# Values of two attention groups made token by token in an fp32 encoder layer, and a weight stream in smaller pieces

## The chip, the core and the metric

The kernel runs on one core of a Trainium2 chip. The core has five engines that run side by side, each with its own fixed list of instructions: TensorE (PE, matrix products), VectorE (DVE), ScalarE (ACT), GpSimd (POOL) and SyncE (SP, which here issues transfers). They wait for each other by semaphores. The metric is the time of one execution on the device in microseconds (us); lower is better.

## What is computed

One layer of a bidirectional encoder over 512 tokens of width 1024, all in fp32. The reference, cut to what the change touches and what ends the kernel:

```python
h = layer_norm(x, ln0_g, ln0_b)
proj = h @ w_in[l] + b_in[l]              # gates B, C, conv input H, and q, k, v
q, k, v = (proj[...].reshape(bsz, seq, N_GROUPS, HEADS_PER_GROUP, HEAD_DIM) for ...)
for g, (window, dil) in enumerate(GROUPS):     # (128,1), (512,4), (2048,16); 8 heads of 64 each
    outs[g], lses[g] = dilated_window_attention(q[:, :, g], k[:, :, g], v[:, :, g], dil, window // (2 * dil), slopes[g])
wts = softmax(stack(lses))                      # the three groups' outputs are merged by their denominators
y_b = sum(wts * outs) @ w_b[l]
mix = (g_a * y_a + g_b * y_b) @ w_o[l] + b_o[l]
h = layer_norm(ALPHA * h + mix, ln1_g[l], ln1_b[l])
f = gelu(dwconv3(a, ffn_conv_w[l]) + ffn_conv_b[l]) * gte      # a, gte = h @ w_up + b_up
h = layer_norm(ALPHA * h + f @ w_down[l] + b_down[l], ln2_g[l], ln2_b[l])
```

## The kernel before

**Products.** An fp32 product is made of three matmuls (`mm3`, L313 to L315): both operands are split into a high and a low part, `hi` and `lo`, and hi·hi, hi·lo and lo·hi are added up in PSUM. `unit` makes 128 features of all 512 tokens: 8 steps of 128 input features, three matmuls each, 24 matmuls of 512 columns.

**Weights.** All weights are one stream of chunks of up to 2048 columns by 128 partitions. `load` (L241) issues a chunk's transfer on SP's queue into one of 2 `raw` buffers; `split` (L250) lets ACT copy it to `hi` (L261) and DVE subtract that copy to get `lo` (L263), 1024 columns at a time (the first two chunks' `lo` are made on POOL). `hi` and `lo` have 3 buffers each, of a chunk's full size. `chunk` splits the chunk that is wanted and the one after it, and loads one more.

**Order.** Each engine's list is arranged when the kernel is built, by a scheduler of the framework that follows the program's order where operands and buffers let it; a buffer that is still being read holds back the instruction that writes it, and what stands behind that one on its engine.

**Attention.** First the tokens are normalised, two tiles of 128 at a time, transposed to features (`hT`) and split. `in_units` then lists the projection in blocks of 128 features: for each of 4 pairs of heads and each of 3 groups a block of queries, keys and values. After each block, `slot` (L597) does a few steps of attention that are due: scores (`Job.a`), scaling by the merge's weights (`Job.b`), transposes of the scores (`Job.b2`), sums over keys (`Job.c`). The values of a block come out with features on partitions, but the sums want keys there: `evac_qkv` copies them to `vT` on ACT (L396 to L399), and `transpose_v` transposes them in four parts on PE (L406), copies the result to a high part (L409) and subtracts for the low part (L410).

**The end.** The gated MLP runs in two parts of the hidden features, with two halves of 512 output columns each. In the last (part 1, half 1), the three chunks of `w_down`, in the stream the numbers 79, 80 and 81, are all kept (`ws`), and the four rows (tiles of 128 tokens, `hb0` to `hb3`) are done one after the other: 11 steps `f11` to `f21` of products, an addition to the row (L809), statistics (L810 and `ln_finish`, L286 to L294), the norm in two steps (L815, L816) and the output's transfer (L817). The last row is done in two parts of 256 columns.

Of the kernel before, what the change touches and what calls it, by code (L numbers as in the profile page):

```python
# [5 lines left out]
F32 = mybir.dt.float32  # L6
# [5 lines left out]
P = 128  # L12
# [66 lines left out]
def lay_out_weights(w):  # L79
    """The weights as one stream of [128, columns] pieces; only moves elements."""  # L80
# [9 lines left out]
    for name, key, cols in chunk_plan():  # L90
        if name == "in":
            c = [block(w_in, units[key + i][3] * P, P) for i in range(2)]
        elif name == "wa":
# [41 lines left out]
def distance_tables():  # L135
    """-(distance) of query (partition) and key (column), MASKED where not attended to."""
# [10 lines left out]
def build(tc, x, wst, colt, dist, rows, out):  # L147
# [3 lines left out]
    with ExitStack() as ctx:  # L151
        pool = lambda name, bufs=1, **k: ctx.enter_context(tc.tile_pool(name=name, bufs=bufs, **k))
        const = pool("const")
        wraw = pool("wraw", 2)
        whl = pool("whl", 3)
        blkp = pool("blk", 25)
# [43 lines left out]
        def first_raw(i, c):  # L200
            if i not in raws:
                raws[i] = wraw.tile([P, 2048], F32, tag="raw", name=f"raw{i}")
            src = wst[i * P * 2048 : (i + 1) * P * 2048].rearrange("(p c) -> p c", p=P)
            first_load(raws[i][:, c : c + 1024], src[:, c : c + 1024])
# [18 lines left out]
        # keys of a pair of heads, block diagonal: rows of head h are zero outside of [:, h]  # L223
# [17 lines left out]
        def load(i):  # L241
# [3 lines left out]
            t = wraw.tile([P, 2048], F32, tag="raw", name=f"raw{i}")  # L245
            src = wst[int(offs[i]) : int(offs[i + 1])].rearrange("(p c) -> p c", p=P)
            nc.sync.dma_start(out=t[:, :n], in_=src)
            raws[i] = t

        def split(i):  # L250
# [5 lines left out]
            lo = whl.tile([P, 2048], F32R, tag="lo", name=f"lo{i}")  # L256
            step = 512 if i == 0 else 1024
            starts = (0, 1024, 512, 1536) if i == 0 else range(0, n, step)
            for c in starts:
                part = slice(c, min(c + step, n))  # L260
                nc.scalar.activation(hi[:, part], raws[i][:, part], AF.Copy)  # L261
                eng = nc.gpsimd if i < 2 else nc.vector
                eng.tensor_tensor(lo[:, part], raws[i][:, part], f(hi[:, part]), op=ALU.subtract)  # L263
            splits[i] = (hi, lo)
# [17 lines left out]
        def ln_finish(sts_, name):  # L282
# [4 lines left out]
            # 1/sqrt(v): the square root's table, then one Newton step  # L287
# [29 lines left out]
        def unit(o, w, c0, rhs, t0=0, t1=512):  # L317
            """o[128 features, tokens] = the block of weights at column c0, times rhs."""
# [43 lines left out]
        def nat(ap):  # L362
            """Token columns in the order (r, i) as seen in a tile whose columns are tokens 4i + r."""
# [48 lines left out]

        class Job:
            """Two heads times 512 columns of scores: a query tile and its window of 256 keys
            (group 0), or two residue classes of 128 queries and as many keys."""
# [69 lines left out]
            def c(self):  # L485
                """Adds to the sums over keys; rows of one head are of use in its own columns."""
                p, g, n = self.key
                v = vv[p, g]
# [351 lines left out]
```

## Time and profile before

| | |
|---|---|
| time, median of 3 runs | 1008.33 us (1007.52 to 1009.56) |
| span of the one profiled execution | 1004.4 us |
| PE busy | 974.7 us, 97% of the span, 4729 matmuls |
| DVE busy | 551.0 us, 55% |
| ACT busy | 398.2 us, 40% |
| POOL busy | 70.2 us, 7% |
| read from HBM, written | 93.84 MB, 2.15 MB |

The time of a run holds a few microseconds that the profiled span does not. Busy shares are means over stages that are limited by different engines. In the rows further down, "out<-in" names the tiles that an instruction writes and reads, L is the line of the kernel, and what stands after "idle before" or in brackets is the time the engine stood still and what ended it.

### The profile page before, as it was taken

The numbers are of one execution on the slowest core, as the hardware profiler recorded it, in microseconds if no ns is written. First come the engines' busy times: TensorE is split into PE (matmuls) and PEld (weight loads), VectorE is DVE, ScalarE is ACT, GpSimd is POOL, SyncE is SP. The second block draws the span as 40 slices with busy tenths as digits, with TensorE's granted clock in tenths as the row PEclk, the third lists the DMA queues.
The fourth block names the chain that finished last, engine by engine and source line by source line (L and its number), as shares of the span: only waits on it lengthen the run. The fifth ranks groups of instructions, "written<-read, shape, count | busy, mean of one in ns | idle before, by whom it ended". The sixth has DMA issues, their size and how long they took to land.

```text
span 1004.4 us, 11766 instructions
## 1 busy us (share of the span) xinstructions
PE 974.7 (97%) x4729; PEld 821.6 (82%) x4729; DVE 551.0 (55%) x863; ACT 398.2 (40%) x679; POOL 70.2 (7%) x161
## 2 busy tenths in 40 slices
PE   7999999999999999999999997799999999999996
PEld 7988888888888888888888886688888888888885
DVE  7856658657675445322355769664542345445256
ACT  4655564564543333233343223254442234444220
POOL 4000000000000000000000304400000000000000
PEclk9999999999999999999999997799999999999998
DMA  6322322122322212225243420232232322321402
GB/s 231 127 87 85 83 81 70 58 85 84 85 85 85 84 59 110 84 84 206 87 138 110 171 84 6 80 126 84 87 112 74 107 103 89 121 84 73 157 1 84
DMA packets 23462, 96.74 MB, mean 96 GB/s; under 512 B 9200, under 2 KB 9584, under 8 KB 13680
## 3 DMA queue, kind: packets, MB, share of 16 engines
q1 hardware_dynamic: 14256, 89.60, 25.6%
q0 software_dynamic: 1728, 6.29, 1.8%
q10 hardware_dynamic: 7424, 0.10, 0.4%
q8 instruction: 37, 0.61, 0.3%
q14 instruction: 17, 0.14, 0.0%
HBM read 93.84 MB, written 2.15 MB: 96 GB/s over the span
## 4 chain that ended last, share of the span: by engine, by line
PE 86%; DVE 8%; DMA 2%; ACT 2%; issue 1%; ACTq 0%; DVEq 0%
PE ps_acc L313 15%; PE ps_acc L314 15%; PE ps_acc L315 15%; PE ps_s L313 5%; PE ps_s L315 5%; PE ps_s L314 5%; PE ps_u L313 5%; PE ps_u L314 5%; PE ps_u L315 5%; PE ps_pt L313 4%; PE ps_pt L315 4%; PE ps_pt L314 4%; DMA s<-st 1%; DVE h1T L310 1%; PE ps_pt L479 1%; DVE h1T L309 1%
## 5 line engine op out<-in xcount | busy, mean ns | idle before, releaser
L263 DVE TENSOR_TENSOR lo<-raw,hi 128x1024 fp32r<-128x1024 f32 (+1 forms) x160 | 190.6, 1211 | 185.1 <-ACT hi L261 183.5
L261 ACT ACTIVATE hi<-raw 128x1024 fp32r<-128x1024 f32 (+1 forms) x166 | 166.6, 1033 | 231.0 <-PE ps_acc L314 67.5
L313 PE MATMUL ps_acc<-hT,hi 128*128 128x512 f32 (+1 forms) x512 | 198.6, 388 | 1.2 <-DVE kbd L392 0.9
L314 PE MATMUL ps_acc<-hT,hi 128*128 128x512 f32 (+1 forms) x512 | 196.7, 384 | 0.1
L315 PE MATMUL ps_acc<-hT,lo 128*128 128x512 f32 (+1 forms) x512 | 196.5, 384 | 0.0
L313 PEld LDWEIGHTS ps_acc<-hT,hi 128*128 128x128 f32 x512 | 96.5, 189 | 20.4 <-PE ps_pt L479 1.6
L315 PEld LDWEIGHTS ps_acc<-hT,lo 128*128 128x128 f32 x512 | 96.4, 188 | 19.2
L314 PEld LDWEIGHTS ps_acc<-hT,hi 128*128 128x128 f32 x512 | 96.5, 189 | 17.7 <-DVE hT L310 0.3
L460 ACT ACTIVATE S<-S,nm 128x128 f32<-128x128 f32 (+2 forms) x96 | 40.1, 419 | 54.3 <-DVE nm L458 47.5
L566 DVE SCALAR_TENSOR_TENSOR cv<-fp,cols,cv 128x512 f32<-128x512 f32 x22 | 16.5, 752 | 72.2 <-ACT cv L565 72.2
L314 PE MATMUL ps_acc<-h1T,hi 128*128 128x512 f32 (+1 forms) x96 | 38.3, 398 | 10.5 <-DVE h1T L310 5.9
L313 PE MATMUL ps_acc<-h1T,hi 128*128 128x512 f32 (+1 forms) x96 | 37.3, 389 | 3.2 <-DVE h1T L309 3.2
L315 PE MATMUL ps_acc<-h1T,lo 128*128 128x512 f32 (+1 forms) x96 | 37.1, 387 | 0.0
L314 PE MATMUL ps_s<-h1T,hi 128*128 128x512 f32 (+1 forms) x96 | 36.3, 378 | 0.0
L313 PE MATMUL ps_s<-h1T,hi 128*128 128x512 f32 (+1 forms) x96 | 36.3, 378 | 0.0
L315 PE MATMUL ps_s<-h1T,lo 128*128 128x512 f32 (+1 forms) x96 | 36.2, 377 | 0.0
L314 PE MATMUL ps_u<-h1T,hi 128*128 128x512 f32 (+1 forms) x96 | 35.7, 372 | 0.0
L315 PE MATMUL ps_pt<-h1T,lo 128*128 128x512 f32 (+1 forms) x96 | 35.7, 372 | 0.0
L314 PE MATMUL ps_pt<-h1T,hi 128*128 128x512 f32 (+1 forms) x96 | 35.7, 372 | 0.0
L313 PE MATMUL ps_u<-h1T,hi 128*128 128x512 f32 (+1 forms) x96 | 35.7, 372 | 0.0
L313 PE MATMUL ps_pt<-h1T,hi 128*128 128x512 f32 (+1 forms) x96 | 35.7, 372 | 0.0
L315 PE MATMUL ps_u<-h1T,lo 128*128 128x512 f32 (+1 forms) x96 | 35.7, 372 | 0.0
(371 smaller groups left out, 1945.7 us busy)
## 6 DMA issues: line engine op xcount, KB each, us to landing
raw<-wst SPq DMA_DIRECT2D x76, 1024.0 KB, 4.8
raw<-wst SPq DMA_DIRECT2D x4, 768.0 KB, 4.2
x<-x SPq DMA_DIRECT2D x4, 512.0 KB, 6.4
raw<-wst SPq DMA_DIRECT2D x4, 512.0 KB, 8.5
hb<-x POOLq DMA_DIRECT2D x4, 512.0 KB, 4.4
out<-hb SPq DMA_DIRECT2D x7, 256.0 KB, 2.1
ln_g<-rows POOLq DMA_DIRECT2D x3, 512.0 KB, 4.2
ln_b<-rows POOLq DMA_DIRECT2D x3, 512.0 KB, 5.4
```

Of the source, the lines that this page charges most:

```text
L261: nc.scalar.activation(hi[:, part], raws[i][:, part], AF.Copy)
L263: eng.tensor_tensor(lo[:, part], raws[i][:, part], f(hi[:, part]), op=ALU.subtract)
L309: nc.vector.tensor_copy(dst[:, 0, c0:c1], t)
L310: nc.vector.tensor_tensor(dst[:, 1, c0:c1], t, f(dst[:, 0, c0:c1]), op=ALU.subtract)
L313: nc.tensor.matmul(o, ah, bh, start=start, stop=False)
L314: nc.tensor.matmul(o, ah, bl, start=False, stop=False)
L315: nc.tensor.matmul(o, al, bh, start=False, stop=stop)
L460: nc.scalar.activation(v, v, AF.Exp, bias=nm[:, j : j + 1], scale=0.125, accum_out=dn[:, j : j + 1])
L479: nc.tensor.transpose(pt[:, j * P : (j + 1) * P], self.pe[:, j * P : (j + 1) * P], ident)
L566: nc.vector.scalar_tensor_tensor(a, u[:, 128:640], col(c + step), a, op0=ALU.mult, op1=ALU.add)
```

## The change

Four things. The values of groups 1 and 2 no longer come from blocks of features: `values` holds 128 tokens of `hT` still and moves 512 weight columns through, so that a group's values for all 8 heads come out with tokens on partitions, 4 tiles for each group. Their weights are two chunks `vt` for each group, behind the 4th and the 6th chunk pair of the projection (`V_AFTER`). `evac_values` adds a bias that is broadcast over partitions (`vbias`, loaded once on POOL's queue), copies and subtracts; nothing is transposed. Second, `raw` becomes 3 buffers of 1024 columns, `lo` becomes 5 buffers of 1024 (`Pieces` finds the piece for a column); `hi` keeps 3 buffers of 2048. A chunk of 2048 columns is loaded in two transfers. Third, `slot` counts in `ready` when a pair's sums are due, and takes newly made scores (`late`) at once rather than from the next slot on. Fourth, there are slots for the new tiles, and one more at the values of group 0 from the second pair on.

```diff
 def in_units():
...
             for kind, base in (("q", BLK_Q), ("k", BLK_K), ("v", BLK_V)):
-                units.append((kind, p, g, base + g * 4 + p))
+                if kind != "v" or g == 0:
+                    units.append((kind, p, g, base + g * 4 + p))
...
+V_AFTER = {4: 1, 6: 2}
...
-    out = [("in", i, 2048) for i in range(0, len(in_units()), 2)]
+    out = []
+    for i in range(0, len(in_units()), 2):
+        out.append(("in", i, 2048))
+        if i in V_AFTER:
+            out += [("vt", (V_AFTER[i], kh), 2048) for kh in range(2)]
...
+class Pieces:
+    def __init__(self, tiles):
+        self.tiles = tiles
+    def __getitem__(self, at):
+        rows, cols = at
+        t = self.tiles[cols.start // 1024]
+        c = cols.start % 1024
+        assert c + cols.stop - cols.start <= 1024
+        return t[rows, c : c + cols.stop - cols.start]
...
-        wraw = pool("wraw", 2)
+        wraw = pool("wraw", 3)
         whl = pool("whl", 3)
-        blkp = pool("blk", 25)
+        blkp = pool("blk", 28)
...
-            t = wraw.tile([P, 2048], F32, tag="raw", name=f"raw{i}")
             src = wst[int(offs[i]) : int(offs[i + 1])].rearrange("(p c) -> p c", p=P)
-            nc.sync.dma_start(out=t[:, :n], in_=src)
-            raws[i] = t
+            raws[i] = []
+            for c in range(0, n, 1024):
+                t = wraw.tile([P, 1024], F32, tag="raw", name=f"raw{i}")
+                nc.sync.dma_start(out=t[:, : min(1024, n - c)], in_=src[:, c : min(c + 1024, n)])
+                raws[i].append(t)
...
-            lo = whl.tile([P, 2048], F32R, tag="lo", name=f"lo{i}")
+            los = [whl.tile([P, 1024], F32R, tag="lo", name=f"lo{i}", bufs=5) for _ in range(0, n, 1024)]
...
+        vbias = blk(F32, (2, 512), "vbias")
+        nc.gpsimd.dma_start(out=vbias.rearrange("p a b -> p (a b)"), in_=vrow.partition_broadcast(P))
+        def values(g, j, ws):
+            o = ps("acc")
+            ts = slice(j * P, (j + 1) * P)
+            for k in range(KT):
+                w, b = ws[k // 4], slice(k % 4 * 512, k % 4 * 512 + 512)
+                mm3(o, hT[k][:, 0, ts], hT[k][:, 1, ts], w[0][:, b], w[1][:, b], k == 0, k == KT - 1)
+            return o
+        def evac_values(g, j, o):
+            a = f32t("vsum")
+            nc.vector.tensor_tensor(a, o, vbias[:, g - 1], op=ALU.add)
+            t = blk(F32R, (2, 4, P), f"vt{g}{j}")
+            nc.scalar.activation(t[:, 0], a.rearrange("p (a b) -> p a b", a=4), AF.Copy)
+            nc.vector.tensor_tensor(t[:, 1], a.rearrange("p (a b) -> p a b", a=4), f(t[:, 0]), op=ALU.subtract)
+            vtok[g, j] = t
...
-            if sums and sums[0].key[0] in cs and wait[0] == 0:
+            if sums and ready[sums[0].key[0]] <= wait[0]:
...
+            scores.extend(late)
+            late.clear()
             if scores:
...
-                    wait[0] = 3
+                    ready[p] = wait[0] + 3
...
-            wait[0] = max(0, wait[0] - 1)
-            scores.extend(late)
-            late.clear()
+            wait[0] += 1
...
             slot()
+            if kind == "v" and a0 > 0:
+                slot()
...
+            if n - 1 in V_AFTER:
+                g = V_AFTER[n - 1]
+                ws = [chunk("vt", (g, kh)) for kh in range(2)]
+                for j in range(4):
+                    o = values(g, j, ws)
+                    slot()
+                    evac_values(g, j, o)
```

Three places of the order are shown; the number behind a name tells tiles of one name apart, and the lines of the changed kernel are other ones (L342 to L344 for L313 to L315, L868 for L809, L874 for L815, L292 for L263).

PE at the end, before: the last products of row 0 (`ps_acc`) with the last chunk's `hi81` and `lo81`, and the first of row 1 (`ps_s`).

```order
L315 MATMUL ps_acc_7193<-hi81_7185,f20_6933 128x512
L313 MATMUL ps_acc_7193<-hi81_7185,f21_7006 128x512
L314 MATMUL ps_acc_7193<-lo81_7186,f21_7006 128x512
L315 MATMUL ps_acc_7193<-hi81_7185,f21_7006 128x512
L313 MATMUL ps_s_7246<-hi79_7125,f11_6276 128x512
L314 MATMUL ps_s_7246<-lo79_7126,f11_6276 128x512
L315 MATMUL ps_s_7246<-hi79_7125,f11_6276 128x512
```

PE at the end, after: the last part of row 3 (`ps_acc_7594`), and in it the last pairs of row 0 (`ps_acc_7399`), 1 (`ps_s`), 2 (`ps_pt`) and of the first part of row 3 (`ps_u`).

```order
L342 MATMUL ps_acc_7594<-hi79_7324,f14_6667 128x256
L343 MATMUL ps_acc_7594<-lo79_7326,f14_6667 128x256
L344 MATMUL ps_acc_7594<-hi79_7324,f14_6667 128x256
L343 MATMUL ps_acc_7399<-lo81_7392,f21_7199 128x512
L344 MATMUL ps_acc_7399<-hi81_7390,f21_7199 128x512
L343 MATMUL ps_s_7452<-lo81_7392,f21_7199 128x512
L344 MATMUL ps_s_7452<-hi81_7390,f21_7199 128x512
L343 MATMUL ps_pt_7505<-lo81_7392,f21_7199 128x512
L344 MATMUL ps_pt_7505<-hi81_7390,f21_7199 128x512
L343 MATMUL ps_u_7558<-lo81_7392,f21_7199 128x256
L344 MATMUL ps_u_7558<-hi81_7390,f21_7199 128x256
L342 MATMUL ps_acc_7594<-hi80_7379,f15_6743 128x256
```

Before, a row's three matmuls with `f21` stand together and the next row follows. After, a row's last two stand behind those that read `lo79` last.

DVE at the end, before: the split of the last chunk, and row 0 (`hb0`).

```order
L263 TENSOR_TENSOR lo81_7186<-raw81_7183,hi81_7185 128x1024
L263 TENSOR_TENSOR lo81_7186<-raw81_7183,hi81_7185 128x512
L809 TENSOR_TENSOR hb0_4330<-hb0_4330,ps_acc_7193 128x512
L810 BN_STATS l20st_7191<-hb0_4330 128x6
L286 BN_AGGR l20mv_7229<-l20st_7191 128x2
L289 TENSOR_SCALAR l20mv_7229<-l20mv_7229 128x1
L815 SCALAR_TENSOR_TENSOR hb0_4330<-hb0_4330,l20mv_7229,ln2_g_7173 128x512 x2
L804 BN_STATS l22st_7297<-hb2_4474 128x6
L290 RECIPROCAL l20mv_7229<-l20mv_7229 128x1
```

DVE at the same place after:

```order
L292 TENSOR_TENSOR lo80_7381<-raw80_7333,hi80_7379 128x1024
L774 TENSOR_TENSOR hb3_4643<-hb3_4643,ps_u_7205 128x512
L292 TENSOR_TENSOR lo81_7391<-raw81_7386,hi81_7390 128x1024
L292 TENSOR_TENSOR lo81_7392<-raw81_7388,hi81_7390 128x512
L868 TENSOR_TENSOR hb0_4418<-hb0_4418,ps_acc_7399 128x512
L868 TENSOR_TENSOR hb1_4493<-hb1_4493,ps_s_7452 128x512
L869 BN_STATS l20st_7397<-hb0_4418 128x6
L869 BN_STATS l21st_7450<-hb1_4493 128x6
L315 BN_AGGR l20mv_7435<-l20st_7397 128x2
L868 TENSOR_TENSOR hb2_4568<-hb2_4568,ps_pt_7505 128x512
L318 TENSOR_SCALAR l20mv_7435<-l20mv_7435 128x1
L874 SCALAR_TENSOR_TENSOR hb0_4418<-hb0_4418,l20mv_7435,ln2_g_7375 128x512 x2
```

The `lo81` piece that was made ahead of row 0 is now in two tiles, and rows 0 to 2 follow each other directly, where before row 0 was finished first.

DVE at the start, before: statistics of the second pair of token tiles (`l01mv`), their norm (`x2`, `x3`), the third chunk's `lo2`, and the first features' split (`hT0`).

```order
L289 TENSOR_SCALAR l01mv_357<-l01mv_357 128x2
L290 RECIPROCAL l01mv_357<-l01mv_357 128x2
L291 TENSOR_TENSOR l01mv_357<-l01mv_357 128x2
L292 TENSOR_TENSOR l01mv_357<-l01mv_357 128x2
L293 TENSOR_SCALAR l01mv_357<-l01mv_357 128x2
L294 TENSOR_TENSOR l01mv_357<-l01mv_357 128x2
L304 TENSOR_SCALAR x2_82<-x2_82,l01mv_357 128x1024
L304 TENSOR_SCALAR x3_83<-x3_83,l01mv_357 128x1024
L263 TENSOR_TENSOR lo2_296<-raw2_189,hi2_295 128x1024 x2
L309 CAST hT0_147<-lnT_374 128x256
```

DVE at the start, after:

```order
L318 TENSOR_SCALAR l01mv_366<-l01mv_366 128x2
L292 TENSOR_TENSOR lo2_302<-raw2_193,hi2_301 128x1024
L319 RECIPROCAL l01mv_366<-l01mv_366 128x2
L320 TENSOR_TENSOR l01mv_366<-l01mv_366 128x2
L321 TENSOR_TENSOR l01mv_366<-l01mv_366 128x2
L322 TENSOR_SCALAR l01mv_366<-l01mv_366 128x2
L323 TENSOR_TENSOR l01mv_366<-l01mv_366 128x2
L333 TENSOR_SCALAR x2_82<-x2_82,l01mv_366 128x1024
L333 TENSOR_SCALAR x3_83<-x3_83,l01mv_366 128x1024
L338 CAST hT0_149<-lnT_383 128x256
L339 TENSOR_TENSOR hT0_149<-lnT_383,hT0_149 128x256
```

One `lo2` piece stands inside the statistics, and the other is no longer ahead of `hT0`.

## Rows read from the trace of the kernel before

**Rows 1.** The page: PE's busy row, and its granted clock by slice.

```profile
PE 974.7 (97%) x4729; PEld 821.6 (82%) x4729; DVE 551.0 (55%) x863; ACT 398.2 (40%) x679; POOL 70.2 (7%) x161
...
PEclk9999999999999999999999997799999999999998
```

**Rows 2.** Windows: busy time of each engine in five stretches, the instructions in brackets.

```profile
140.00:300.00 160.00, 158.22 (x819) 133.98 (x818) 107.99 (x217) 85.95 (x204) 2.05 (x14) 1.00 0.24 76
300.00:600.00 300.00, 300.00 (x1377) 250.30 (x1376) 141.84 (x168) 99.74 (x132) 18.72 (x37) 1.00 0.31 110
600.00:650.00 50.00, 36.30 (x209) 32.15 (x208) 41.66 (x66) 12.29 (x23) 22.07 (x11) 0.80 0.12 43
650.00:973.00 323.00, 323.00 (x1456) 269.03 (x1456) 142.69 (x164) 121.41 (x152) 15.15 (x86) 1.00 0.27 95
973.00:1004.40 31.40, 23.11 (x134) 20.30 (x132) 21.95 (x58) 1.18 (x4) 0.00 (x0) 0.91 0.18 67
```

**Rows 3.** The chain that ended last, around 60 us: start, length, engine, tile, line.

```profile
59.80 0.23 PE ps_acc L313
...
61.16 0.44 PE ps_pt L406 x4
61.60 0.12 PE ps_s L313
```

**Rows 4.** Groups by line: values' transposes, last step; busy, mean ns | idle.

```profile
L410 DVE TENSOR_TENSOR v<-ps_pt,v 128x512 fp32r<-128x512 f32 x12 | 8.3, 688 | 9.9 <-ACT v L409 9.8
...
L406 PE MATMUL ps_pt<-cols,vT 128*128 128x128 f32 x48 | 7.2, 273 | 0.6 <-ACT vT L397 0.6
```

**Rows 5.** The page's DMA issues: 1 MB loads, us to landing.

```profile
raw<-wst SPq DMA_DIRECT2D x76, 1024.0 KB, 4.8
```

**Rows 6.** Waits of the queue of loads: what for, us in total, times, longest.

```profile
SPq L247 <- DVE lo L263: 853.0, 73, 32.8
```

**Rows 7.** Timeline of POOL at the start: start us, busy us, instruction.

```profile
18.22 5.46 POOL L263 TENSOR_TENSOR lo<-raw,hi 128x1024 fp32r<-128x1024 f32 x2 [3.41 <-ACT hi L261]
```

**Rows 8.** Timeline of DVE in the first 50 us.

```profile
21.73 2.27 DVE L289 TENSOR_SCALAR l01mv<-l01mv 128x2 f32<-128x2 f32 x1
...
24.85 1.54 DVE L304 TENSOR_SCALAR x<-x,l01mv 128x1024 f32<-128x1024 f32 x2
26.30 2.35 DVE L263 TENSOR_TENSOR lo<-raw,hi 128x1024 fp32r<-128x1024 f32 x2
...
40.80 3.50 DVE L263 TENSOR_TENSOR lo<-raw,hi 128x1024 fp32r<-128x1024 f32 x3
```

**Rows 9.** Timeline of PE: the first transposes of values, idle time ahead in brackets.

```profile
41.69 0.66 PE L406 MATMUL ps_pt<-cols,vT 128*128 128x128 f32 x4 [0.64 <-ACT vT L397]
```

**Rows 10.** Timeline of POOL in the middle, at the norm.

```profile
607.53 2.40 POOL L756 TENSOR_TENSOR hb<-hb,ln_g 128x1024 f32<-128x1024 f32 x1 [30.49 <-PE ps_pt L733]
```

**Rows 11.** Timeline of DVE in the same stretch.

```profile
612.75 2.39 DVE L309 CAST h1T<-lnT 128x256 fp32r<-128x256 f32 x1
...
623.03 1.21 DVE L263 TENSOR_TENSOR lo<-raw,hi 128x1024 fp32r<-128x1024 f32 x1
...
624.50 0.67 DVE L715 TENSOR_TENSOR hb<-hb,ps_u 128x512 f32<-128x512 f32 x1
```

**Rows 12.** Timeline of DVE in the last 20 us, from the third row's addition.

```profile
988.24 0.69 DVE L809 TENSOR_TENSOR hb<-hb,ps_pt 128x512 f32<-128x512 f32 x1 [1.68 <-PE ps_pt L315]
...
990.00 0.74 DVE L815 SCALAR_TENSOR_TENSOR hb<-hb,l22mv,ln_g 128x512 f32<-128x512 f32 x1
...
990.74 0.73 DVE L815 SCALAR_TENSOR_TENSOR hb<-hb,l22mv,ln_g 128x512 f32<-128x512 f32 x1
...
993.48 0.41 DVE L809 TENSOR_TENSOR hb<-hb,ps_u 128x256 f32<-128x256 f32 x1
...
996.14 0.42 DVE L809 TENSOR_TENSOR hb<-hb,ps_acc 128x256 f32<-128x256 f32 x1 [1.79 <-PE ps_acc L315]
...
999.55 1.54 DVE L816 SCALAR_TENSOR_TENSOR hb<-hb,l23mv,ln_b 128x512 f32<-128x512 f32 x3
```

More of the change, by code (lines that the diff above doesn't have):

```diff
@@ L92, in lay_out_weights @@
             c = [block(w_in, units[key + i][3] * P, P) for i in range(2)]
+        elif name == "vt":
+            g, kh = key
+            c = [block(w_in[kh * 512 : (kh + 1) * 512], (BLK_V + g * 4) * P, 512)]
         elif name == "wa":
@@ L144, in distance_tables, with build @@
     return np.ascontiguousarray(np.concatenate(t, axis=1).astype(np.float32))
-def build(tc, x, wst, colt, dist, rows, out):
+class Pieces:
[7 more added lines that the diff above has]
+        return t[rows, c : c + cols.stop - cols.start]
+def build(tc, x, wst, colt, dist, rows, vrow, out):
     from contextlib import ExitStack
@@ L200, in first_raw @@
         def first_raw(i, c):
-            if i not in raws:
-                raws[i] = wraw.tile([P, 2048], F32, tag="raw", name=f"raw{i}")
+            raws.setdefault(i, [])
+            raws[i].append(wraw.tile([P, 1024], F32, tag="raw", name=f"raw{i}"))
             src = wst[i * P * 2048 : (i + 1) * P * 2048].rearrange("(p c) -> p c", p=P)
-            first_load(raws[i][:, c : c + 1024], src[:, c : c + 1024])
+            first_load(raws[i][-1], src[:, c : c + 1024])
         first_load(xt[0], xr[0])
@@ L260, in split @@
                 part = slice(c, min(c + step, n))
-                nc.scalar.activation(hi[:, part], raws[i][:, part], AF.Copy)
+                raw, lo = (t[c // 1024][:, c % 1024 :][:, : part.stop - c] for t in (raws[i], los))
+                nc.scalar.activation(hi[:, part], raw, AF.Copy)
                 eng = nc.gpsimd if i < 2 else nc.vector
-                eng.tensor_tensor(lo[:, part], raws[i][:, part], f(hi[:, part]), op=ALU.subtract)
-            splits[i] = (hi, lo)
+                eng.tensor_tensor(lo, raw, f(hi[:, part]), op=ALU.subtract)
+            splits[i] = (hi, Pieces(los))
         where = {(c[0], c[1]): i for i, c in enumerate(plan)}
@@ L411, in transpose_v @@
             vv[p, g] = t
+        vbias = blk(F32, (2, 512), "vbias")
+        nc.gpsimd.dma_start(out=vbias.rearrange("p a b -> p (a b)"), in_=vrow.partition_broadcast(P))
+        vtok = {}
+        def values(g, j, ws):
[12 more added lines that the diff above has]
+            vtok[g, j] = t
         class Job:
@@ L487, in c @@
                 p, g, n = self.key
-                v = vv[p, g]
+                v = vv.get((p, g))
                 key = (p, 0, n // 2) if g == 0 else (p, 1, n)
@@ L501, in c @@
                     for i in range(2):
-                        j, cc = 2 * n + i, slice(i * 256, (i + 1) * 256)
-                        mm3(u[:, cc], v[:, 0, j], v[:, 1, j], hi[:, cc], lo[:, cc], g == 1 and i == 0, g == 2 and i == 1)
+                        cc, vt = slice(i * 256, (i + 1) * 256), vtok[g, 2 * n + i]
+                        mm3(u[:, cc], vt[:, 0, p], vt[:, 1, p], hi[:, cc], lo[:, cc], g == 1 and i == 0, g == 2 and i == 1)
                 if p not in ctmp:
@@ L593, in build @@
         vtodo, late, scores, sums, scaled, running = [], [], [], [], [], []
-        wait = [0]
+        wait, ready = [0], {}
         def slot():
@@ L831 @@
         "rows": np.ascontiguousarray(np.stack([w[k].reshape(-1) for k in ROWS])),
+        "vrow": np.ascontiguousarray(w["b_in"][:, (BLK_V + 4) * P : (BLK_V + 12) * P]),
     }
```

## The prediction

> **What bounds the kernel now.** The page's first part comes first: TensorE (PE) is busy 974.7 us of a span of 1004.4 us, at a granted clock of nearly full speed, except in three of the 40 slices [rows 1]. So a change pays where it takes work off PE or fills one of PE's gaps, and it costs where it makes a new gap. The windows say where gaps are [rows 2]: from 300 to 600 us and from 650 to 973 us PE is busy without a break; in the attention from 140 to 300 us it idles 160.00 − 158.22 = 1.8 us; around the norm in the middle, 600 to 650 us, 13.7 us; and in the last 31.4 us it idles 8.3 us, most of it after its last matmul, when VectorE (DVE) finishes the last row of tokens. Matmuls of 512 columns follow each other after (61.16 − 59.80) / 6 = 0.227 us, and those of 256 after 0.12 us [rows 3]. All this is one profiled execution. Its span stands 3.9 us under the median of the runs, 1008.33; I add terms to the span and keep the 3.9.
>
> **Values by tokens.** The matmuls that make the values are 8 × 24 of 512 columns before and after, so PE gains nothing there. Gone are 8 × 4 transposes: four of them hold PE for 0.44 us in the chain [rows 3], so 8 × 0.44 = **−3.5 us**, all of it in stretches where PE sets the pace. One transpose alone is listed as lasting 0.273 us [rows 4]; four in a row overlap, so I take 0.11 each and keep 32 × 0.273 = 8.7 us as the other end.
>
> The Trainium skill, "TensorE: Matmul & The Clock Gate", Part 4 (PE-mode transpose), gives about 275 ns for a 128x128 transpose inside a kernel; by it the removal would be worth an estimated 32 × 0.275 = 8.8 us and the sum would end near 1014.2. The listed duration agrees, but the chain's spacing does not, and the spacing is what PE loses.
>
> DVE changes little. An add of the bias (0.69, as the subtraction of the old evacuation [rows 4]) comes for each of 8 new tiles: 5.5 us more on DVE and as much less on ScalarE (ACT). DVE is busy 107.99 us of 160 there [rows 2], and each new tile has 24 × 0.227 = 5.45 us of matmuls to cover its evacuation, with two accumulators in turn. I take 0 for the rest of the attention. Its lower bound is −1.8 (all of PE's idle time there goes); for a loss I take as much again and one evacuation of 0.69 in the way, +2.5.
>
> **Half-size loads.** The stream is loaded in 160 pieces of at most 512 KB where there were 80 of at most 1 MB. A 1 MB load lands in 4.8 us [rows 5], and the queue of loads waited 853 us for DVE to give a buffer back [rows 6]: transfers are covered by the wait for room, and I price the smaller ones at 0. Without that cover, each late piece would cost its landing, 4.8 us, and two splits of some 1.2 us: 7.2 us.
>
> The Trainium skill, "DMA: Bandwidth & Descriptors", Measured, asks for DMAs of 1 MiB or more to reach three quarters of the peak, which speaks against the halves. By it the loads would be slower, yet only the 853 us of waiting would shrink; the sum stays.
>
> **The start.** Three things move. First, on DVE one `lo2` piece (1.2 us, half of the pair's 2.35) now stands inside the statistics of the second pair of token tiles, where DVE and GpSimd (POOL) already hold each other up: one tiny TENSOR_SCALAR there takes 2.27 us beside POOL's two `lo` pieces [rows 7, 8]. The second pair's normalisation ends at some 28.0 us rather than 26.39 [rows 8]; the other `lo2` piece moves behind the casts of the features, which gives part of it back: by my count of the rows in between the transposes lose 1.0 us and the first matmuls 0.7. Second, PE waited 0.64 us for the old `vT` of group 0 [rows 9]; scores now go first: −0.64. Third, the extra slot and the early `late` list put a third score block ahead of the next projection. It waits for the buffer of the first block, which DVE frees only behind the `lo` pieces that run from 40.80 to 44.30 us [rows 8]: an estimated +1.2, the length of one piece, and 0.2 at the fourth block. Sum 0.7 − 0.64 + 1.4 = **+1.4 us**; ends −0.8 (only the vanished wait and its neighbours count) and +2.5.
>
> **The middle.** While POOL's 1024-wide operations run, from 607.53 us on, DVE's small operations take 2.4 us each [rows 10, 11]. In the order after, the second `lo48` piece stands between the features' casts of this stretch (five buffers of 1024 columns hold less than three of 2048), the first `lo49` piece goes behind the last feature, and an add of 0.67 comes ahead of it. A piece takes 1.21 us undisturbed [rows 11]; in and out cancel roughly, the add and a bit of interference stay: **+0.8 us**, with one turn of 2.4 us either way as bounds.
>
> **The tail decides.** All three `dn` chunks of the last stage stay live through its four rows of tokens. They need 2 + 2 + 2 = 6 `lo` pieces; the pool has 5. So `lo81_7392`, the second piece of the last chunk, can be written only when `lo79_7325` has been read for the last time, which is in the last 256 columns of the last row. The order shows it: each row stops two matmuls short of its end, one with `lo` and one with `hi`, and the four closing pairs stand together, the first of them 29 matmuls from PE's end. Before, row by row came ready, 33 matmuls of 0.227 = 7.5 us apart, and DVE took each in 993.48 − 988.24 = 5.24 us while PE worked on the next [rows 12]. That cover is gone: all four rows come to DVE at once.
>
> - When they start: 29 matmuls stand behind the restart, 6 of 512 columns and 23 of 256: 6 × 0.227 + 23 × 0.12 = 4.1 us. The row's first pair takes 0.45 of it, and PE waits an estimated 0.2 to 0.3 us for the `lo` piece, which delays what follows; so the first add begins some 3.5 us ahead of the old last one: 996.14 − 3.5 = 992.65 us.
> - How long DVE takes: one behind the other, 3 × 5.24 for three rows, 2 × 0.73 for statistics of first halves that were done earlier before, 0.9 for the first 256 columns of row 3, and the old end after PE, 999.55 + 1.54 − 996.14 = 4.95: 23.0 us. But rows can now fill each other's waits: two 512-wide operations start 0.74 us apart with a tiny one between them [rows 12], so that tiny ones in between cost 0.08 rather than the 0.2 of one that waits for the one ahead of it; so counted, about 20.4 us.
> - The end of DVE is then 992.65 + 20.4 to 23.0 = 1013.0 to 1015.7, where it was 1001.09: +11.9 to +14.6. Since the order after does mix rows 0, 1 and 2, I take a value near the lower end, **+12.5 us**. The last output's transfer (1001.09 to the span's end) stays behind it.
>
> **Sum:** −3.5 + 1.4 + 0 + 0.8 + 12.5 = +11.2: a span of 1015.6 us and a time of **1019.5 us**. The tail's ends, with 1 to 2 us from start and middle, give 1016 to 1022.5 for this case.
>
> **Rivals.**
> - *The tail is covered anyway.* If PE's closing pairs came early enough that DVE met the rows nearly as before, only −3.5 + 1.4 + 0.8 = −1.3 would remain: 1007.0 us, not slower. For it: DVE is idle 9.4 of the last 31.4 us [rows 2]. Against: that idle time is waiting for PE, and the fixed order leaves 29 matmuls (some 4 us) as cover for three rows of 5.24. It decides once the tail costs less than 1.3 + 2 = 3.3 us. Chance 0.05.
> - *The new chunks starve PE.* Each value group wants two whole chunks at once from smaller pools. One late piece is 7.2 us, so 1026.7; both groups 1033.9. For: four of five `lo` pieces are held by a group. Against: a group runs 4 × 5.45 us on them, long against a landing. Chance 0.08. The rule of the Trainium skill's page on DMA, named above, would make it likelier.
> - *The middle shifts by turns.* One or two turns of 2.4 us beside POOL: 1021.9 to 1024.3, or 1014.7 to 1017.1. For: what sets that stretch is which DVE operation meets which POOL one [rows 10, 11], and one has moved. Against: of what stands in this stretch only those three move. Chance 0.12.
> - *Transposes are worth their listed duration:* 8.7 where I take 3.5, so 1014.3. Against: 0.44 for four [rows 3]. Chance 0.05. The Trainium skill's page on TensorE, named above, has nearly the same figure.
>
> **How the numbers follow.** The forecast has 0.70. The range 1014 to 1024 takes in it, the transposes' case and the middle's: 0.87 by these chances. It leaves out the covered tail and the starved PE. A measurement tells some 0.2% (2 us) from no change; the covered tail, at −1.3, is within that, mostly: same 0.04, faster 0.02, slower 0.94.
>
> **What would show it.** After PE's last matmul the profile should have some 15 to 17 us of DVE (now 4.95); PE's last four closing pairs should come together; the last additions to rows 0 and 1 should start within a microsecond or two of each other near PE's end. PE's busy time should fall by about 3.5 us; 300 to 600 us should stay without a gap. The start is right if PE reaches its first full-width projection 1 to 2 us later. The prediction is wrong if the rows are finished one by one as now, or if PE waits for `hi` or `lo` in the attention.

## The result and the profile after

The changed kernel takes 1018.28 us (median of 4 runs, 1016.62 to 1019.49) where the kernel before, in the same series, took 1008.2: a ratio of 1.0098, 95% interval 1.0084 to 1.0112. It is 10.1 us slower; the forecast was 1019.5 us, 11.2 us slower. The span of the profiled execution is 1017.4 us.

The page's rows on PE, as in [rows 1]:

```profile
PE 972.1 (96%) x4697; PEld 819.3 (81%) x4697; DVE 561.6 (55%) x871; ACT 394.9 (39%) x671; POOL 80.3 (8%) x162
...
PEclk8999999999999999999999997799999999999996
```

PE is busy 2.6 us less, for 3.5 forecast, and its last slice is emptier (2 tenths for 6 on the page before). The windows (columns as in [rows 2]):

```profile
140.00:300.00 160.00, 157.83 (x821) 134.80 (x820) 113.28 (x231) 89.95 (x219) 2.69 (x12) 0.99 0.24 70
236.00:239.40 3.40, 3.40 (x14) 3.00 (x13) 2.93 (x8) 2.20 (x6) 0.00 (x0) 0.51 0.56 155
300.00:600.00 300.00, 300.00 (x1370) 249.96 (x1369) 141.64 (x167) 98.90 (x130) 21.01 (x38) 1.00 0.33 111
600.00:650.00 50.00, 35.60 (x206) 31.43 (x205) 40.90 (x65) 12.42 (x23) 22.18 (x11) 0.82 0.13 42
...
973.00:1017.40 44.40, 25.12 (x141) 21.81 (x139) 20.10 (x59) 1.18 (x4) 0.00 (x0) 0.81 0.13 48
```

From 300 to 600 us PE is busy without a gap, as before. The last stage was 31.4 us with 23.1 us of PE; now it is 44.4 with 25.1. The second row is a short stretch with a granted clock of 0.51; the last section is about it. DVE's timeline shows the start, the middle and the tail:

```profile
10.10 1.18 DVE L323 TENSOR_TENSOR l00mv<-l00mv 128x2 f32<-128x2 f32 x1
11.32 3.39 DVE L333 TENSOR_SCALAR x<-x,l00mv 128x1024 f32<-128x1024 f32 x2
...
26.41 1.21 DVE L292 TENSOR_TENSOR lo<-raw,hi 128x1024 fp32r<-128x1024 f32 x1
...
618.55 3.35 DVE L292 TENSOR_TENSOR lo<-raw,hi 128x1024 fp32r<-128x1024 f32 x1
...
992.98 0.69 DVE L292 TENSOR_TENSOR lo<-raw,hi 128x512 fp32r<-128x512 f32 x1 [23.08 <-PE ps_acc L343]
994.50 0.69 DVE L868 TENSOR_TENSOR hb<-hb,ps_acc 128x512 f32<-128x512 f32 x1 [0.83 <-PE ps_acc L344]
995.10 0.68 DVE L868 TENSOR_TENSOR hb<-hb,ps_s 128x512 f32<-128x512 f32 x1
...
997.00 0.63 DVE L868 TENSOR_TENSOR hb<-hb,ps_pt 128x512 f32<-128x512 f32 x1
...
1007.21 0.41 DVE L868 TENSOR_TENSOR hb<-hb,ps_u 128x256 f32<-128x256 f32 x1
...
1007.61 0.41 DVE L868 TENSOR_TENSOR hb<-hb,ps_acc 128x256 f32<-128x256 f32 x1
...
1012.53 1.54 DVE L875 SCALAR_TENSOR_TENSOR hb<-hb,l23mv,ln_b 128x512 f32<-128x512 f32 x3
```

In the tail all is as the order had it. The last `lo` piece waits 23.08 us for PE (992.98). Then the last additions to rows 0, 1 and 2 start at 994.50, 995.10 and 997.00, where [rows 12] has a whole row of tokens between two of them. DVE needs 1012.53 + 1.54 − 994.50 = 19.57 us from the first of them to its end. PE's timeline after, at three places that both kernels have (the first transposes of `x`, the first projection of full width, and transposes of `hb` behind the middle) and at two new waits between them:

```profile
13.09 0.47 PE L374 MATMUL ps_pt<-cols,x 128*128 128x128 f32 x1 [6.07 <-DVE x L333]
...
46.69 0.47 PE L342 MATMUL ps_s<-kbd,q 128*128 128x512 f32 x1 [1.21 <-DVE S L503]
...
47.47 0.39 PE L342 MATMUL ps_acc<-hT,hi 128*128 128x512 f32 x1
...
235.64 0.39 PE L342 MATMUL ps_u<-PT,vt 128*128 128x256 f32 x1 [2.04 <-ACT PT L531]
...
236.71 0.63 PE L343 MATMUL ps_acc<-hT,hi 128*128 128x512 f32 x1
237.13 0.41 PE L343 MATMUL ps_u<-PT,vt 128*128 128x256 f32 x1
...
637.33 0.44 PE L792 MATMUL ps_acc<-cols,hb 128*128 128x128 f32 x2
```

PE's timeline of the kernel before at the three common places:

```profile
10.83 0.33 PE L345 MATMUL ps_pt<-cols,x 128*128 128x128 f32 x1 [3.02 <-DVE x L304]
...
43.41 0.39 PE L313 MATMUL ps_acc<-hT,hi 128*128 128x512 f32 x1
...
635.59 0.44 PE L733 MATMUL ps_acc<-cols,hb 128*128 128x128 f32 x2
```

PE waits nowhere for `hi` or `lo` in the attention, so the rival of the starved PE is out. With the first and the last of these places the difference of the spans, 13.0 us, can be split. PE's first transposes come 13.09 − 10.83 = 2.3 us later; from there to the transposes at 637.33 the new kernel needs 624.24 us, the old one 624.76, so it gains 0.5; from there to DVE's end it takes 1014.07 − 637.33 = 376.74 us, the old one 1001.09 − 635.59 = 365.50, so the tail costs **11.2 us**. The 2.3 us need not be the change's: profiles of kernels with either order there begin those transposes anywhere from 10.8 to 13.1 us (last section). The spans' 13.0 and the times' 10.1 agree too: in the runs that have both on record the time is 1.7 to 1.9 us above the span, so the profiled execution of the kernel before took an estimated 1006.2 us, 2.1 below its median (they are in the 3.9 that I counted as time outside the span), and the one profiled here, 1019.17 us, is 0.9 above its own.

### The profile page after: what moved, and what is told of

It reads as the page before. It is cut to its first block, busy times and chain, and to the rows that moved or that the text cites. A ratio compares the mean times of both kernels' runs of the same rounds, so it can differ in the third digit from the quotient of the medians.

```text
span 1017.4 us, 11949 instructions
## 1 busy us (share of the span) xinstructions
PE 972.1 (96%) x4697; PEld 819.3 (81%) x4697; DVE 561.6 (55%) x871; ACT 394.9 (39%) x671; POOL 80.3 (8%) x162
## 4 chain that ended last, share of the span: by engine, by line
PE 88%; DVE 8%; ACT 1%; issue 1%; DMA 0%; DVEq 0%
PE ps_acc L343 15%; PE ps_acc L342 15%; PE ps_acc L344 15%; PE ps_s L342 5%; PE ps_s L343 5%; PE ps_s L344 5%; PE ps_u L342 5%; PE ps_u L343 5%; PE ps_u L344 5%; PE ps_pt L342 4%; PE ps_pt L344 4%; PE ps_pt L343 4%; PE ps_pt L529 1%; DVE h1T L339 1%; DVE lo L292 1%
## 5 line engine op out<-in xcount | busy, mean ns | idle before, releaser
L292 DVE TENSOR_TENSOR lo<-raw,hi 128x1024 fp32r<-128x1024 f32 (+1 forms) x160 | 195.6, 1224 | 267.3 <-ACT hi L290 99.4
L342 PE MATMUL ps_acc<-hT,hi 128*128 128x512 f32 (+1 forms) x448 | 173.2, 387 | 0.0
L343 PE MATMUL ps_acc<-hT,hi 128*128 128x512 f32 (+1 forms) x448 | 171.8, 384 | 0.0
L344 PE MATMUL ps_acc<-hT,lo 128*128 128x512 f32 (+1 forms) x448 | 171.4, 383 | 0.0
L344 PEld LDWEIGHTS ps_acc<-hT,lo 128*128 128x128 f32 x448 | 84.3, 188 | 16.5
L342 PEld LDWEIGHTS ps_acc<-hT,hi 128*128 128x128 f32 x448 | 84.5, 189 | 15.5
L343 PEld LDWEIGHTS ps_acc<-hT,hi 128*128 128x128 f32 x448 | 84.4, 188 | 15.5 <-DVE hT L339 0.2
L342 PE MATMUL ps_acc<-h1T,hi 128*128 128x512 f32 (+1 forms) x96 | 37.3, 388 | 3.1 <-DVE h1T L338 3.1
L344 PE MATMUL ps_acc<-h1T,lo 128*128 128x512 f32 (+1 forms) x96 | 37.1, 387 | 0.0
L342 PE MATMUL ps_s<-h1T,hi 128*128 128x512 f32 (+1 forms) x96 | 36.3, 378 | 0.0
L344 PE MATMUL ps_s<-h1T,lo 128*128 128x512 f32 (+1 forms) x96 | 36.2, 377 | 0.0
L342 PE MATMUL ps_pt<-h1T,hi 128*128 128x512 f32 (+1 forms) x96 | 35.7, 371 | 0.0
L344 PE MATMUL ps_pt<-h1T,lo 128*128 128x512 f32 (+1 forms) x96 | 35.7, 371 | 0.0
L344 PE MATMUL ps_u<-h1T,lo 128*128 128x512 f32 (+1 forms) x96 | 35.6, 371 | 0.0
L342 PE MATMUL ps_u<-h1T,hi 128*128 128x512 f32 (+1 forms) x96 | 35.6, 371 | 0.0
L343 PEld LDWEIGHTS ps_acc<-h1T,hi 128*128 128x128 f32 x96 | 19.3, 201 | 15.6 <-DVE h1T L339 12.3
```

What stands on the lines that cost most here:

```text
L292: eng.tensor_tensor(lo, raw, f(hi[:, part]), op=ALU.subtract)
L342: nc.tensor.matmul(o, ah, bh, start=start, stop=False)
L343: nc.tensor.matmul(o, ah, bl, start=False, stop=False)
L344: nc.tensor.matmul(o, al, bh, start=False, stop=stop)
```

## Experiments

Each is compared with the kernel before in five rounds on one chip. The table gives all; "without a fix" means that the last stage still has five pieces. A difference counts where an interval leaves 1 out, or where two kernels' intervals stay apart.

| kernel | us | ratio to before, 95% interval |
|---|---|---|
| own_last | 1006.91 | 0.9984 (0.9976 to 0.9993) |
| pieces_only, without a fix | 1017.85 | 1.0091 (1.0078 to 1.0104) |
| pieces_own | 1006.27 | 0.9976 (0.9967 to 0.9986) |
| twice_t | 1014.58 | 1.0065 (1.0053 to 1.0077) |
| lo6_b27 | 1011.35 | 1.0028 (1.0018 to 1.0039) |
| lo6_t11 | 1013.36 | 1.0043 (1.0030 to 1.0056) |
| lo6_t11_pool | 1009.96 | 1.0010 (1.0001 to 1.0018) |
| no_slot | 1010.47 | 1.0022 (1.0012 to 1.0032) |
| late_old | 1006.50 | 0.9981 (0.9973 to 0.9990) |
| both_old_pool | 1009.04 | 1.0003 (0.9993 to 1.0012) |
| full_own | 1005.73 | 0.9973 (0.9963 to 0.9982) |
| full_late | 1005.46 | 0.9968 (0.9957 to 0.9979) |

**The tail alone (own_last).** One piece of 82 chunks gets another buffer; the orders of PE and DVE differ from the changed kernel's in the last stage alone, those of the other engines not at all.

```diff
-            los = [whl.tile([P, 1024], F32R, tag="lo", name=f"lo{i}", bufs=5) for _ in range(0, n, 1024)]
+            los = [(blkp if i == 81 and c else whl).tile([P, 1024], F32R, tag="blk" if i == 81 and c else "lo", ...) for c in range(0, n, 1024)]
```

> The changed kernel, with one edit: the sixth lo piece of the last stage has a buffer of its own, so that nothing waits there for a piece to be given back; all else keeps its order on every engine. Theory (the tail alone costs the change its time: in the two traces DVE's end moved by 11.3 us against PE's stage before it): the time falls by 11.3 us from 1018.3 to about 1007.0 us, and DVE works some 5 us after PE's last matmul. Rival (the rows would come to DVE together anyway, or PE gets slower in the last stage for its other orders): the time stays above 1013 us.

It took 1006.91 us: 11.4 us less than the changed kernel. DVE's last rows, the last addition and the end:

```profile
996.68 0.42 DVE L868 TENSOR_TENSOR hb<-hb,ps_acc 128x256 f32<-128x256 f32 x1 [1.78 <-PE ps_acc L344]
...
1000.09 1.54 DVE L875 SCALAR_TENSOR_TENSOR hb<-hb,l23mv,ln_b 128x512 f32<-128x512 f32 x3
```

From the last addition to the end are 4.95 us, as in [rows 12]; the three rows before it are done by then. The loss is the tail, and the tail is the missing buffer.

**The pieces without the values (pieces_only, pieces_own).** The kernel before with `Pieces`, 3 `raw` and 5 `lo` buffers, and its old values; in the second with own_last's edit as well.

```diff
-        wraw = pool("wraw", 2)
+        wraw = pool("wraw", 3)
...
-            lo = whl.tile([P, 2048], F32R, tag="lo", name=f"lo{i}")
+            los = [whl.tile([P, 1024], F32R, tag="lo", name=f"lo{i}", bufs=5) for _ in range(0, n, 1024)]
```

> The kernel before with the smaller pieces alone (3 raw and 5 lo buffers of 1024 columns, loads of 512 KB), values still by features with transposes. Theory (a transpose costs PE its spacing of 0.11 us, the values' new way is worth 3.5 us, and the pieces carry all of the loss): about 3.5 us above the changed kernel, 1021.8 us, with the same tail of 15 to 16 us after PE's last matmul. Rival (a transpose is worth its listed 0.27 us): 8.7 us above, 1027 us. Rival (the values' new way is worth nothing, since waits take its place): 1018 us.

> The kernel before with the smaller pieces (3 raw and 5 lo buffers of 1024 columns), and in the last stage a buffer of its own for the sixth lo piece; values still by features with transposes. Theory (the pieces' only loss is the tail, and they gave back about 2 us of PE's waits in the attention): 11.3 us less than 1017.85, 1006.5 us, the same as the changed kernel with that buffer, so that the values' new way is worth nothing on balance. Rival (the tail costs less without the values' change, and the new way is worth its 3.5 us): 1010 us.

The first took 1017.85 us, as much as the changed kernel: the rival that the values' new way is worth nothing on balance was right, and my 3.5 us wrong. The second confirms it: 1006.27 us, 11.6 less, and 0.6 below own_last. The pieces alone, once the tail is mended, are 2 us faster than the kernel before. A window of pieces_own shows where most of it comes from:

```profile
140.00:300.00 160.00, 159.57 (x832) 136.28 (x832) 109.40 (x218) 86.78 (x204) 3.15 (x14) 1.00 0.24 73
```

PE is busy 159.57 of these 160 us, for 158.22 in [rows 2]: with the smaller buffers most of PE's waits in this stretch, 1.4 us, are gone.

**The price of a transpose (twice_t).** The kernel before with its 48 transposes done twice.

```diff
-            for w in range(4):
+            for w in (0, 1, 2, 3) * 2:
```

> The kernel before with each of the 48 transposes of values done twice, into the same place: nothing else. It measures the price of a transpose by itself. Theory (0.109 us, their spacing in the trace): 48 x 0.109 = 5.2 us more, 1013.4 us. Rival (the listed duration of 0.273 us): 13.1 us more, 1021.3 us. Rival (PE has room there): no change.

6.0 us more by the medians; the interval, 5.3 to 7.8 us by the ratio, divided by 48 gives 0.11 to 0.16 us for each. It is the spacing of [rows 3], not the listed duration of [rows 4]. The orders of DVE and ACT shift at some places too, but the chain that ended last has the price by itself, eight transposes in 0.87 us:

```profile
63.51 0.87 PE ps_pt L406 x8
```

So, if one taken away is worth what one added costs, PE did save its 3.5 us, and they were given back elsewhere. This kernel has before's order at the start, and its first transposes of `x`:

```profile
12.96 0.47 PE L345 MATMUL ps_pt<-cols,x 128*128 128x128 f32 x1 [5.65 <-DVE x L304]
```

They begin at 12.96 us, as late as in the changed kernel. In the profile after, the cause stands in DVE's timeline: a tiny operation of the statistics at 10.10 us takes 1.18 us beside POOL's first `lo` pieces, where [rows 8] has the same thing later, at 21.73. The last section comes back to it.

**Where the 3.5 us went (no_slot, late_old).** PE has two new waits in the profile after: 1.21 us at 46.69, for the third score block's buffer, and 2.04 us at 235.64, for ACT's copy of PT (the transposed scores), between two slots with no projection in between. Two edits on top of own_last:

```diff
# no_slot
-            if kind == "v" and a0 > 0:
-                slot()
# late_old: the two lines stand at the end of slot() again
-            scores.extend(late)
-            late.clear()
```

> The changed kernel with the sixth lo piece's own buffer in the last stage, and without the extra slot behind the values of group 0 (from the second pair on). Theory (with two slots in a row, the second one's sums want the scores that the first has just transposed, and no projection lies between: PE waited 2.0 us for ACT's copy at 235 us in the trace): PE's wait for PT goes, and the time falls by some 2 us from 1006.9 to 1004.9 us. Rival (the sums then come later and their steps stand uncovered at the end of the attention): 1007 us or more.

> The changed kernel with the sixth lo piece's own buffer in the last stage, and new scores taken from the next slot on, as before the change. Theory (the third score block waits 1.4 us for its buffer at 46.7 us, and the wait of 0.8 us for the first transposes that had vanished comes back): 0.6 us less, 1006.3 us, with PE waiting for vT and no longer for S. Rival (the early scores are worth more later on, since merges are due earlier): 1008 us or more.

late_old came out as forecast, at 1006.50 us (0.4 us below own_last, within the intervals): one wait for another. no_slot was a miss, 1010.47 us. The wait for PT is gone, but PE has these instead (its waits, in all, times, longest):

```profile
PE ps_s L342 <- DVE S L503: 3.3, 2, 2.1
...
PE ps_acc L342 <- ACT Csb L627: 1.9, 1, 1.9
```

In the first line 2.1 us are new and for a score buffer (the rest is the wait for the third score block's, as in own_last). DVE's timeline up to it:

```profile
233.29 1.89 DVE L524 TENSOR_TENSOR S<-S,mrg 128x512 f32<-128x512 f32 x3
235.10 1.89 DVE L524 TENSOR_TENSOR S<-S,c 128x512 f32<-128x512 f32 x3
...
238.64 0.74 DVE L503 SCALAR_TENSOR_TENSOR S<-dtab,ps_s 128x256 f32<-128x256 f32 x2
```

Without the extra slot, DVE does a pair's multiplications by the merge's weights in one go, and the scores that PE waits for stand behind them. So the extra slot pays for itself; the wait that it makes is the smaller one.

**More pieces everywhere (lo6_b27, lo6_t11, lo6_t11_pool).** Six `lo` buffers, with room from one block buffer less (27 for 28) or two temporary buffers less (11 for 13). The third moves a merge's four small transfers from ACT's queue to POOL's.

```diff
-            los = [whl.tile([P, 1024], F32R, tag="lo", name=f"lo{i}", bufs=5) for _ in range(0, n, 1024)]
+            los = [whl.tile([P, 1024], F32R, tag="lo", name=f"lo{i}", bufs=6) for _ in range(0, n, 1024)]
# lo6_t11_pool, four times in merge()
-            nc.scalar.dma_start(
+            nc.gpsimd.dma_start(
```

> The changed kernel with six lo pieces rather than five everywhere (and one block buffer less, to make room). Theory: the tail's 11.3 us go, and the lo piece that stood in the middle stretch beside GpSimd is made earlier, which gives back 0.7 to 1.1 us more: about 1006 us. Rival (the pieces' place in the middle is worth nothing, or one block buffer less costs something): 1007 us or more, as with a sixth buffer in the last stage alone.

> The changed kernel with six lo pieces everywhere, and room made by two temporary buffers less in place of one block buffer. Its order on ACT has the load of the second pair's statistics behind the copies of the keys again, as in the changed kernel, where the other version with six pieces had it ahead of them and ACT stood 8.6 us for that transfer. Theory (that place of one transfer cost the other version its 4.4 us): about 1006 us. Rival (the sixth piece itself costs, by its lo2 piece inside the statistics at the start or otherwise): 1009 us or more.

> The version with six lo pieces and two temporary buffers less (1013.4 us), with one edit: the four small transfers of each merge are issued by GpSimd instead of ACT; PE's order stays the same but for one row. Theory (it was slow because ACT stood 6.9 us at 266 us in its own queue for the landing of a transfer, ahead of exponentials and copies that PE needed, and what followed): those waits of ACT go, and the time falls to about 1006 us. Rival (the sixth piece itself, which is now made inside the statistics at the start and elsewhere earlier, costs the time): it stays above 1011 us.

All three missed, upwards. The tail is mended in each, but the start and the attention are worse. In lo6_b27, ACT's waits show a part of it (in all, times, longest):

```profile
ACT kbd L419 <- DMA s<-st: 8.6, 1, 8.6
```

and its timeline at that wait:

```profile
203.41 0.34 ACTq L583 DMA_DIRECT2D st<-s  x1
203.80 0.68 ACT L419 ACTIVATE kbd<-ps_acc,cols 64x512 fp32r<-64x512 f32 x1 [8.61 <-DMA s<-st]
```

The load of a pair's statistics for the merge (`st<-s`) must wait for the store ahead of it to land, and it stands on ACT's queue. In the changed kernel it comes between two copies of the keys (`kbd`); here it was put ahead of both, so they wait 8.6 us for a transfer they don't need. Of this, two waits of 1.7 and 0.3 us reach PE, at 205 us. In lo6_t11 it is another pair's, ahead of the exponentials, as ACT's timeline shows:

```profile
266.09 0.33 ACTq L583 DMA_DIRECT2D st<-s  x1
266.47 0.40 ACT L510 ACTIVATE S<-S,nm 128x128 f32<-128x128 f32 x1 [6.93 <-DMA s<-st]
```

With the transfers on POOL's queue, lo6_t11 gains 3.4 us of the 7 forecast; these waits of ACT are gone. The rest, 3 us above own_last, is placed in part. Two of PE's waits in this version (in all, times, longest):

```profile
PE ps_pt L374 <- DVE x L333: 7.2, 4, 5.0
...
PE ps_acc L342 <- ACT Csb L627: 2.3, 2, 1.5
```

The first is 5.5 us in own_last; with six pieces both `lo2` pieces stand inside the statistics that the second pair of `x` waits for. PE's first projection of full width, in lo6_t11_pool and then in own_last:

```profile
50.44 0.40 PE L342 MATMUL ps_acc<-hT,hi 128*128 128x512 f32 x1
...
47.55 0.39 PE L342 MATMUL ps_acc<-hT,hi 128*128 128x512 f32 x1
```

Counted from PE's first transposes that is 37.6 us for 34.4, and lo6_t11 (36.5) and lo6_b27 (37.4) have it too. So the sixth piece costs 2 to 3 us by its place at the start, in all three, as one rival had it. The second wait, for a gate's copy on ACT late in the attention, own_last doesn't have. Which buffer brings it stays open.

**The old slots with the new values (both_old_pool).** Both edits of no_slot and late_old, on top of own_last, and the merges' transfers on POOL's queue.

> The values token by token with the smaller pieces and the sixth piece's own buffer in the last stage, but the slots as before the change (no extra slot, new scores from the next slot on), and the merges' transfers issued by GpSimd. Theory (values by tokens save PE 3.5 us, and what took them back was the change of the slots and ACT's waits for the merges' transfers): 3.5 us less than the smaller pieces alone with that buffer, 1006.3, so 1002.8 us, faster than both kernels. Rival (the new tiles' own order costs the attention as much): 1006 us or more.

A miss: 1009.04 us, no faster than the kernel before. PE waits 3.3 us in one place,

```profile
PE ps_s L342 <- DVE S L503: 3.3, 1, 3.3
```

and DVE's timeline up to there:

```profile
242.38 0.69 DVE L524 TENSOR_TENSOR S<-S,c 128x512 f32<-128x512 f32 x1 [1.15 <-DMA c<-s]
...
243.06 1.89 DVE L524 TENSOR_TENSOR S<-S,c 128x512 f32<-128x512 f32 x3
244.86 1.89 DVE L524 TENSOR_TENSOR S<-S,mrg 128x512 f32<-128x512 f32 x3
246.66 1.22 DVE L292 TENSOR_TENSOR lo<-raw,hi 128x1024 fp32r<-128x1024 f32 x1
247.80 0.75 DVE L503 SCALAR_TENSOR_TENSOR S<-dtab,ps_s 128x256 f32<-128x256 f32 x2
```

Seven multiplications of a pair (`S<-S,c` and `S<-S,mrg`), 4.3 us together, and a `lo` piece stand ahead of the score at 247.80 that PE wants, and they could not begin before `c` had landed, 1.15 us of waiting at 242.38. The new values take two blocks out of each pair's nine, and their eight tiles all stand early, behind the sixth and the eighth block of the projection (by the code; "behind the 4th and the 6th chunk pair" was wrong): from then on the attention's steps have seven projections of 5.45 us for a pair to lie beside, and the same transfers to wait for. I take this loss of cover for what cost the 3.5 us: this kernel and no_slot show it in the same form, and the changed kernel's wait for PT fits it. It is argued, not shown: no run gives the steps their two projections back. A rival in this kernel is the new queue: `c` lands 3.0 us after its issue on POOL's queue, and 1.9 to 2.6 us after it in own_last, on ACT's; no run has the old slots without that move.

**Whole loads (full_own, full_late).** own_last with 2 `raw` buffers of 2048 and 80 loads of a whole chunk; the second with late_old's edit too.

```diff
-            for c in range(0, n, 1024):
-                t = wraw.tile([P, 1024], F32, tag="raw", name=f"raw{i}")
-                nc.sync.dma_start(out=t[:, : min(1024, n - c)], in_=src[:, c : min(c + 1024, n)])
-                raws[i].append(t)
+            t = wraw.tile([P, 2048], F32, tag="raw", name=f"raw{i}")
+            nc.sync.dma_start(out=t[:, :n], in_=src)
+            raws[i] = [t[:, c : c + 1024] for c in range(0, n, 1024)]
```

> The changed kernel with the sixth lo piece's own buffer in the last stage, with the weights loaded in 80 whole chunks into 2 raw buffers of 2048 columns, as before the change (one block buffer less, for the room); lo pieces stay. It measures the price of half-size loads. Theory (the queue of loads waits for buffers all the time, so their size is hidden): 1006.9 us, no change. Rival (smaller loads cost by their fixed share): 1005 us or less. Rival (a smaller piece frees its buffer earlier, and that is what helped the attention): 1008 us or more.

> The two edits that did not lose, together: the sixth lo piece's own buffer in the last stage with whole chunks loaded (1005.7), and new scores taken from the next slot on (0.4 us better than without, by 1006.5 against 1006.9). Theory (the two are independent): 1005.3 us, ahead of the kernel before by 0.3%. Rival (each edit of the slots or buffers changes the order in which DVE and ACT meet the merges' transfers, and PE finds a new wait of 2 us or more in the attention): 1007.5 us or more.

full_own took 1005.73 us, 1.2 less than own_last: halves cost little, as forecast, or about a microsecond; the two intervals overlap, so a price is not settled. The 2 us that the pieces gained are still there with whole loads, which leaves the pieces of `lo` as their likely source. full_late took 1005.46 us, 0.3% below the kernel before; its median is the lowest of the study, but its interval overlaps full_own's.

## Why the prediction was right

- **The tail (+12.5)** measured 11.2 us in the trace, 11.4 by own_last and 11.6 by pieces_own. The mechanism is the one forecast. After PE's last matmul DVE works about 16 us, for 15 to 17 forecast. DVE's 19.57 us lie just under the lower end of my 20.4 to 23.0: operations of different rows overlap even more than I counted (the additions to rows 0 and 1, 0.69 us each, start 0.60 apart). The first addition came 3.4 us ahead of the old last one, counted from the transposes behind the middle, for 3.5 forecast.
- **The transposes (−3.5)** were priced rightly: twice_t. The rival with 0.27 us for each is refuted. Doubling 48 transposes cost 0.11 to 0.16 us each. The Trainium skill, "TensorE: Matmul & The Clock Gate", Part 4, gives about 275 ns for a transpose (in bf16) inside a kernel. The listed 273 [rows 4] agree with it, the price for PE does not.
- **The rest of the attention (0)** was right only as a sum. The values' new way with its slots was forecast at −2.7 us (−3.5, −0.64 and +1.4); own_last stands 0.6 above pieces_own, which is nothing or a small loss. Of the difference PE's wait for PT, 2.04 us, is what the rows show; the rest is not placed. And the pieces gained 2 us that I had not seen. The step that failed is the cover: I counted 5.45 us of matmuls over each new tile's evacuation and took 0 for all else, and did not count what the scores, sums and merges beside the later blocks lose. That the loss of cover is the cause is argued, not shown (above).
- **The start (+1.4)**: the third score block waits 1.21 us, as forecast (1.2), and the wait for `vT` has gone. One `lo2` piece stands inside the statistics (26.41). From the span's start on, the spread of 2.3 us there hides the price, but counted from PE's first transposes it shows: the first projection of full width comes after 47.47 − 13.09 = 34.38 us, where it was 43.41 − 10.83 = 32.58, 1.8 us later, for 1 to 2 forecast. Some 0.8 us of that is the third score block's own work (46.69 to 47.47), which only moved ahead; about 1.0 remains of the +1.4.
- **The middle (+0.8)**: from POOL's first operation, 607.53 [rows 10] and 608.61, to the transposes at 635.59 and 637.33 it is 0.7 us longer, and the `lo` piece there takes 3.35 us instead of 1.21 (618.55), a shared turn with POOL. But twice_t, with DVE's order of the kernel before there, needs 28.70 us for the same way, as much as the changed kernel's 28.72 (the kernel before: 28.06); so the 0.7 us are not shown to be the change's.
- **Half-size loads (0)**: full_own puts them at about 1 us, not clear of nothing.

So the tail, the term that decides, was forecast by its mechanism and 1 us too high. That the sum came within 1.2 us is luck: outside the tail the pieces were forecast at +1.5 us (0.7 at the start, 0.8 in the middle) and measured −2.1 (pieces_own against the kernel before in its series, 1008.41 us), and the values with their slots were forecast at −2.7 and measured +0.6, two errors of over 3 us that nearly cancelled.

## What to carry to other kernels

When buffers are cut into smaller ones, count them against the stage that keeps the most of them alive, not against the steady state: one piece short of six reordered every row of the last stage and cost eleven microseconds, though the steady state got better. Work taken off the busiest engine is worth its price only if the engine finds no new waits: here 3.5 us of transposes went and nothing was left of them, most likely because the steps that lay beside the moved work lost their cover. And a transfer on ACT's queue that waited for another transfer held ACT's copies and exponentials behind it for 8.6 and 6.9 us, so its place in that order deserves a look after every change of buffers.

## What the runs showed of the hardware

After the 2.04 us wait at 235.64, PE's granted clock was 0.51 from 236 to 239.4 us, the lower of its two levels (1.2 GHz): a 512-column matmul was followed by the next one after 0.42 us (236.71 to 237.13), and the stretch cost about 1.5 us more than in own_last, where the same wait of 2.04 us at the same place was followed by full clock (PE's timeline, then the window):

```profile
235.71 0.39 PE L342 MATMUL ps_u<-PT,vt 128*128 128x256 f32 x1 [2.04 <-ACT PT L531]
...
236.00:239.40 3.40, 3.40 (x21) 2.95 (x20) 3.37 (x9) 2.28 (x6) 0.00 (x0) 1.00 0.57 160
```

The same wait thus cost 2 us in one execution and 3.5 in another. In the same way the start of the kernel, where DVE and POOL meet, took 2.2 us more in one profile than in another with the same order there: the first transposes of `x` came at 10.91 us in no_slot and at 13.09 in the changed kernel, at 10.83 and 12.96 in the two with before's order. PE and DVE in no_slot:

```profile
10.91 0.33 PE L374 MATMUL ps_pt<-cols,x 128*128 128x128 f32 x1 [3.31 <-DVE x L333]
...
8.89 0.16 DVE L323 TENSOR_TENSOR l00mv<-l00mv 128x2 f32<-128x2 f32 x1
```

The operation that took 1.18 us in the changed kernel (10.10) takes 0.16 here. The 14 profiles fall into three groups by it and the one ahead of it, which take 0.16 or 0.17 us, or 1.1 to 1.3 beside POOL's first `lo` piece: with neither drawn out the transposes begin at 10.8 to 11.1 us (four profiles), with one at 11.8 to 12.0 (three), with both at 12.9 to 13.1 (seven).
